# Order of the first loads and of the last token tile in a two-layer decoder trunk, on one core

## The chip, the core and the metric

The kernel runs on one core of one Trainium2 chip. A core has five engines that run side by side, each with a queue of instructions that it works off in order: TensorE (PE: matrix products, and in a part of its own the loading of the stationary operand, PEld), VectorE (DVE), ScalarE (ACT), GpSimd (POOL) and SyncE (SP, which here only issues transfers). Transfers between the device's memory (HBM) and the on-chip memory (SBUF) can be triggered from SP, ACT and POOL; a trigger is an instruction in that engine's queue. Matrix products land in PSUM, eight banks of 128 x 512 float32.

The metric is the device time of one execution in microseconds (us), as a median over runs. The kernel before was run three times: 1031.11, 1033.86 and 1035.78 us, median 1033.86.

## The reference

One sequence of 512 tokens of width 1024 goes through two layers. The first mixes tokens by a gated convolution, the second by attention in a sliding window; each is followed by a gated feed-forward part (width 2816). All is float32.

```python
def rmsnorm(x, g):
    xf = x.astype(jnp.float32)
    r = lax.rsqrt(jnp.mean(xf * xf, axis=-1, keepdims=True) + EPS)
    return (xf * r).astype(x.dtype) * g

def short_conv_mixer(h, w_in, conv_w, w_out):
    bcx = h @ w_in
    b_gate, c_gate, u = jnp.split(bcx, 3, axis=-1)
    y = b_gate * causal_depthwise_conv3(c_gate * u, conv_w)
    return y @ w_out

def swiglu(h, w_gate_up, w_down):
    g, u = jnp.split(h @ w_gate_up, 2, axis=-1)
    return (jax.nn.silu(g) * u) @ w_down

# layer 0
mix = short_conv_mixer(rmsnorm(h, a_pre_norm[l]), a_w_in[l], a_conv_w[l], a_w_out[l])
h = h + rmsnorm(mix, a_post_norm[l])
# layer 1: keys, values and queries of rmsnorm(h), windowed attention with sinks, then
h = h + rmsnorm(attn, b_post_norm[j])
# each layer ends with
ff = swiglu(rmsnorm(h, ffn_pre_norm[l]), ffn_w_gate_up[l], ffn_w_down[l])
h = h + rmsnorm(ff, ffn_post_norm[l])
```

So every part ends the same way: a mix of 512 x 1024 is divided by its root mean square, multiplied by a weight vector and added to the stream h.

## The kernel before

**Numbers in two halves.** Products are made in a faster type (F32R, a float32 of fewer bits). Each operand is split in a high part (`hi`, an ACT copy into that type) and the rest (`lo`, a DVE subtraction), and three products hi x hi, hi x lo and lo x hi are summed in PSUM (`mm3`, lines 188 to 191). So a weight tile of 128 x 1024 costs one ACT copy and one DVE subtraction before PE can use it, and PE has three products for each tile product.

**The start (lines 211 to 226 and 645 to 677).** The token matrix comes transposed as eight tiles `xt[k]` of 128 features x 512 tokens, the first three weight tiles `first[t]` (128 x 1024 each) in pieces of 2, 2 and 4 blocks of 128 columns (`CUTS`). ACT triggers the first piece of each weight tile, SP all else: `xt[0]`, the small table `gt` of norm gains and convolution taps (32 KB), `xt[1]`, the second pieces, and so on. PE begins with `WARM` = 8 products of a matrix of ones that nobody uses (tile `idle`). ACT loads its function table at a first small activation (`warm`, line 648). Then, for each k, ACT scales and copies `xt[k]` to `xhi` (needs `gt`), DVE makes `xlo`, ACT and DVE split the weight pieces, and PE makes nine products into three PSUM banks, in the order hi x hi for the three weights, then hi x lo, then lo x hi.

**The row factors (lines 680 to 699).** The first norm is applied behind the products. The squares of the tokens give a column `cols` (128 x 4, by POOL's power function); four diagonal matrices `dg` times a matrix of ones, in float32, spread it over all partitions as `pr`, which ACT copies to `rows`.

**A closing (`close`, lines 830 to 866).** The last product of a part, with its weights in slots and its operands (here `ys`), goes over four token tiles t and two halves of 512 columns. An object `Update` holds the mix, the sums of squares `s`, `v`, `r` = v to the power -1/2, the weight vector `G` spread over 128 partitions (512 KB in SBUF) and a scrap tile `junk`. Per tile: `take` (DVE, bank + mix), `square_mix` (ACT), `scale` (DVE, times G), `mean` (DVE and POOL), `update` (DVE, h += mix x r). Then h's own norm (`square`, `mean2`, `norm`), and PE's transposes (`turn`, line 323) of the normed tile `xn`. Between, `ahead.one()` splits four weight tiles of the next part (lines 396 and 401). `Update.load` (line 243) takes two tiles of a pool of 14 (`wide`) and triggers the load of G on SP.

**The last closing (lines 1129 to 1150).** No next part follows. Tiles 0 to 2 are done by halves; in tile 3 the second half is cut in two quarters of 256 columns (`take_quarter`, line 257), so that the work after PE's last product is short. Then `scale`, `update` and the store to `out`.

**What sets the order.** Blocks under `tc.manual_schedule` keep the written order of PE, DVE, ACT and POOL within that block. Across blocks, and for SP, a planner at build time orders the instructions by its own estimate of when they are ready; it also gives tiles their places and puts in the semaphores. Loads triggered by SP and ACT share eight completion semaphores in turn.

Of the kernel before, what the change touches and what calls it, by code (L numbers as in the profile page):

```python
# [16 lines left out]
P = 128  # L17
# [24 lines left out]
WARM = 8  # L42
# [30 lines left out]
def yoco_kernel(  # L73
# [67 lines left out]
    nc.vector.memset(mhalf, -0.5)  # L141
    gt = const.tile([P, N_GAIN], F32, name="gt")
# [71 lines left out]
    CUTS = [(0, 2), (2, 4), (4, KT)]  # L214
    for t in range(3):
        nc.scalar.dma_start(first[t][:, : CUTS[0][1] * P], w_in[0, t, :, : CUTS[0][1] * P])
    for k in range(KT):
        nc.sync.dma_start(xt[k], xT[k])
        if k == 0:
            nc.sync.dma_start(gt, gains)  # L220
        for k0, k1 in CUTS[1:]:
            if k == k0 - 1:
                for t in range(3):
                    nc.sync.dma_start(first[t][:, k0 * P : k1 * P],
                                      w_in[0, t, :, k0 * P : k1 * P])
# [3 lines left out]
    class Update:  # L229
# [27 lines left out]
        def take_quarter(self, t, c, ps):  # L257

            m = self.mix[t][:, S + c : S + c + 256]
            nc.vector.tensor_tensor(out=m, in0=ps[:, :256], in1=m, op=ALU.add)  # L260
            i = 2 * t + (c > 0)
            if c:
                self.scale(t, 0)
                nc.vector.tensor_scalar(out=self.s[:, i - 1 : i], in0=self.s[:, i - 1 : i],
                                        scalar1=self.s[:, 8:9], scalar2=EPS, op0=ALU.add,
                                        op1=ALU.add)
            nc.scalar.activation(self.junk[:, c : c + 256], m, AF.Square, scale=1 / 32,
                                 accum_out=self.s[:, i : i + 1] if c else self.s[:, 8:9])
            if c:
                nc.vector.tensor_scalar(out=self.v[:, t : t + 1], in0=self.s[:, i : i + 1],  # L270
                                        scalar1=self.s[:, i - 1 : i], scalar2=None, op0=ALU.add)
                nc.gpsimd.tensor_tensor(out=self.r[:, t : t + 1], in0=self.v[:, t : t + 1],
                                        in1=mhalf[:, :1], op=ALU.pow)

        def scale(self, t, half):
            c = slice(half * S, (half + 1) * S)
            m = self.mix[t][:, c]
            nc.vector.tensor_tensor(out=m, in0=m, in1=self.G[:, c], op=ALU.mult)
# [366 lines left out]
    with tc.manual_schedule(engines=ALL):  # L645
# [6 lines left out]
        for k in range(KT):  # L652
            hi, lo = xs[k]
            nc.scalar.activation(hi, xt[k], AF.Copy, scale=g(G_APRE, k))
            nc.vector.scalar_tensor_tensor(
                out=lo, in0=xt[k], scalar=g(G_APRE, k), in1=hi.bitcast(F32),
                op0=ALU.mult, op1=ALU.subtract,
            )
            for k0, k1 in CUTS:
                if k == max(k0 - 1, 0):  # L660
                    kk = slice(k0 * P, k1 * P)
                    for t in range(3):
                        hi, lo = ws[t]
                        nc.scalar.activation(hi[:, kk], first[t][:, kk], AF.Copy)
                        nc.vector.tensor_tensor(
                            out=lo[:, kk], in0=first[t][:, kk], in1=hi[:, kk].bitcast(F32),
                            op=ALU.subtract,
                        )
            kk = slice(k * P, (k + 1) * P)
            xhi, xlo = xs[k]  # L670
            for i in range(3):
# [876 lines left out]
```

## Time and profile before

| | |
|---|---|
| three runs, us | 1031.11, 1033.86, 1035.78 |
| median, us | 1033.86 |
| the profiled execution's own time: its span, us | 1031.2 |
| mean granted TensorE clock, share of full | 0.998 |
| DMA | 244.59 MB, mean 237 GB/s |
| bytes from HBM / to HBM | 237.15 MB / 102.76 MB |

The page of the profile counts one execution from its first to its last instruction (the span). A row of a timeline has the start in us, the duration in us, the engine, the line, the operation, what is written and read, the shapes and the count; in brackets how long the engine stood idle before it and what ended that. `L673` is line 673 of the kernel. `PEq`, `SPq` and `ACTq` are an engine's sequencer, which issues transfers. A list of waits has the waiting engine and line, what it waited for, the sum in us, how often, and the longest. The chain of waits follows the work that ended last back to its releasers. A group of a line's instructions has shortest, median and longest duration in ns.

### The profile page before, as it was taken

How to read it: one execution, taken by the hardware profiler on the slowest of the kernel's cores; microseconds unless marked ns; L12 is line 12 of the kernel's file. 1: busy time of each engine (PE TensorE's matmuls, PEld its weight loads, DVE VectorE, ACT ScalarE, POOL GpSimd, SP SyncE). 2: the span in 40 equal slices, each digit the busy share in tenths (PEclk: the TensorE clock that was granted, in tenths of full speed). 3: DMA queues.
4: the chain of work that ended last, by engine and by line, in shares of the span. 5: the costliest groups of instructions: out<-in, count | busy, mean ns of one | idle time of the engine just before them, and what ended most of it. 6: DMA issues, size and time to landing. Idle time of an engine off the chain costs nothing.

```text
span 1031.2 us, 17486 instructions
## 1 busy us (share of the span) xinstructions
PE 1018.6 (99%) x6652; PEld 927.2 (90%) x6652; DVE 820.9 (80%) x1397; ACT 577.4 (56%) x1037; POOL 196.8 (19%) x259
## 2 busy tenths in 40 slices
PE   9999999999999999999999999999999999999997
PEld 7888887999999899999898888889998999989986
DVE  5666766888777978878869998688886788887786
ACT  7222543865656354566466777668565554645632
POOL 0433132102101021000122664221111010210001
PEclk9999999999999999999999999999999999999999
DMA  9897689548978789869504879975899676998732
GB/s 334 290 250 235 184 261 332 160 164 256 328 243 277 254 282 301 284 209 308 190 1 135 214 216 275 256 254 164 263 284 327 177 255 203 312 293 256 244 134 82
DMA packets 66868, 244.59 MB, mean 237 GB/s; under 512 B 7904, under 2 KB 8800, under 8 KB 55008
## 3 DMA queue, kind: packets, MB, share of 16 engines
q1 hardware_dynamic: 51616, 146.34, 38.8%
q0 software_dynamic: 14592, 96.48, 36.6%
q8 instruction: 52, 0.85, 0.3%
q10 hardware_dynamic: 576, 0.66, 0.2%
q14 instruction: 32, 0.26, 0.1%
HBM read 237.15 MB, written 102.76 MB: 330 GB/s over the span
## 4 chain that ended last, share of the span: by engine, by line
PE 91%; DVE 4%; DMA 2%; ACT 1%; issue 1%; POOL 0%; POOLq 0%; SPq 0%; DVEq 0%; ACTq 0%
PE gx L191 7%; PE gx L190 7%; PE gx L189 7%; PE gz L191 4%; PE gz L190 4%; PE gz L189 4%; PE px L189 4%; PE px L191 4%; PE pcub L191 4%; PE px L190 4%; PE pcub L189 4%; PE pcub L190 4%; PE pmix L191 2%; PE pmix L189 2%; PE pmix L190 2%; PE gy L191 2%
## 5 line engine op out<-in xcount | busy, mean ns | idle before, releaser
L455 DVE TENSOR_TENSOR wlo<-raw,whi 128x1024 fp32r<-128x1024 f32 x225 | 274.9, 1226 | 93.4 <-ACT whi L454 93.3
L454 ACT ACTIVATE whi<-raw 128x1024 fp32r<-128x1024 f32 x225 | 234.5, 1050 | 120.6 <-DVE raw L442 22.0
L189 PE MATMUL gx<-xt,whi 128*128 128x256 f32 x480 | 135.8, 283 | 0.0
L190 PE MATMUL gx<-xt,whi 128*128 128x256 f32 x480 | 135.8, 283 | 0.0
L191 PE MATMUL gx<-xt,wlo 128*128 128x256 f32 x480 | 135.8, 283 | 0.0
L523 POOL DMA_DIRECT2D hsum<-in_w_gb_dram x96 | 63.2, 743 | 160.5 <-ACT whi L454 82.3
L189 PEld LDWEIGHTS gx<-xt,whi 128*128 128x128 f32 x480 | 92.2, 192 | 0.0
L190 PEld LDWEIGHTS gx<-xt,whi 128*128 128x128 f32 x480 | 92.2, 192 | 0.0
L191 PEld LDWEIGHTS gx<-xt,wlo 128*128 128x128 f32 x480 | 92.2, 192 | 0.0
L973 ACT ACTIVATE st<-gx 128x256 f32<-128x256 f32 x80 | 30.1, 382 | 81.2 <-PE gx L191 81.2
L523 POOL DMA_DIRECT2D hsum<-hsum x32 | 25.2, 788 | 258.8 <-ACT whi L454 192.3
L189 PE MATMUL pcub<-xlo,whi 128*128 128x512 f32 x168 | 65.4, 390 | 0.0
L191 PE MATMUL pcub<-xhi,wlo 128*128 128x512 f32 x168 | 65.4, 389 | 0.0
L190 PE MATMUL pcub<-xhi,whi 128*128 128x512 f32 x168 | 65.3, 389 | 0.0
L191 PE MATMUL px<-whi,alo 128*128 128x512 f32 x120 | 46.7, 389 | 0.0
L190 PE MATMUL px<-whi,ahi 128*128 128x512 f32 x120 | 46.7, 389 | 0.0
L189 PE MATMUL px<-wlo,ahi 128*128 128x512 f32 x120 | 46.7, 389 | 0.0
L191 PE MATMUL gx<-xhi,wlo 128*128 128x256 f32 x160 | 45.3, 283 | 0.0
L189 PE MATMUL gy<-xlo,whi 128*128 128x256 f32 x160 | 45.3, 283 | 0.0
L190 PE MATMUL gy<-xhi,whi 128*128 128x256 f32 x160 | 45.3, 283 | 0.0
L191 PE MATMUL gy<-xhi,wlo 128*128 128x256 f32 x160 | 45.3, 283 | 0.0
L189 PE MATMUL gz<-xt,whi 128*128 128x256 f32 x160 | 45.3, 283 | 0.0
(262 smaller groups left out, 3118.3 us busy)
## 6 DMA issues: line engine op xcount, KB each, us to landing
hsum<-in_w_gb_dram POOLq DMA_DIRECT2D x96, 512.0 KB, 8.0
raw<-hsum SPq DMA_DIRECT2D x88, 512.0 KB, 8.1
raw<-in_w_gb_dram SPq DMA_DIRECT2D x60, 512.0 KB, 7.5
hsum<-in_w_dn_dram POOLq DMA_DIRECT2D x36, 512.0 KB, 8.6
raw<-in_w_dn_dram SPq DMA_DIRECT2D x32, 512.0 KB, 7.0
hsum<-hsum POOLq DMA_DIRECT2D x28, 512.0 KB, 5.3
raw<-in_w_in_dram SPq DMA_DIRECT2D x21, 512.0 KB, 7.5
hsum<-in_w_dn_dram POOLq DMA_DIRECT2D x12, 768.0 KB, 12.2
```

Of the source, the lines that this page charges most:

```text
L189: nc.tensor.matmul(out, whi, xlo, start=start, stop=False, **kw)
L190: nc.tensor.matmul(out, whi, xhi, start=False, stop=False, **kw)
L191: nc.tensor.matmul(out, wlo, xhi, start=False, stop=stop, **kw)
L454: self.begun = nc.scalar.activation(hi[:, :n], raw, AF.Copy)
L455: nc.vector.tensor_tensor(out=lo[:, :n], in0=raw, in1=hi[:, :n].bitcast(F32), op=ALU.subtract)
L523: nc.gpsimd.dma_start(dst, src, max_dma_last_dim=4 * 4 * S, **kw))
L973: nc.scalar.activation(s, x, AF.Copy)
```

## The change

- First loads: `gt` is triggered by POOL ahead of all else on that engine. ACT triggers five weight pieces (the three first, two of the second) and not three; `xt[1]` and `xt[2]` go ahead of SP's other pieces.
- Warming: ten idle products and not eight.
- First k-tile: the weights' first block (128 columns) is split by itself, ahead of the second, and the nine products of k = 0 have an order of their own, with two lo x hi products ahead of the hi x lo ones.
- Row factors: the four diagonals stand in one tile, which is split in two parts; two products of 512 columns with a matrix of ones in the faster type replace four in float32.
- First closing: `res.load` moves into the closing's block, ahead of its work, and triggers G on ACT's queue.
- Last token tile: `update` of tile 2 moves into tile 3, in two halves behind the take of the first half and that of the first quarter; the first half's `scale` of tile 3 goes to POOL; the last quarter's sum of squares is one DVE instruction that starts from the sum so far, in place of an ACT square and a DVE sum.

```diff
-WARM = 8
+WARM = 10
...
+    gt = const.tile([P, N_GAIN], F32, name="gt")
+    nc.gpsimd.dma_start(gt, gains)
     ident = const.tile([P, P], F32, name="ident")
     make_identity(nc, ident)
     ones = const.tile([P, P], F32, name="ones")
     nc.vector.memset(ones, 1.0)
+    ones_r = const.tile([P, P], F32R, name="ones_r")
+    nc.vector.memset(ones_r.bitcast(F32), 1.0)
...
+    def piece(queue, t, c):
+        c = slice(CUTS[c][0] * P, CUTS[c][1] * P)
+        queue.dma_start(first[t][:, c], w_in[0, t, :, c])
+
     for t in range(3):
-        nc.scalar.dma_start(first[t][:, : CUTS[0][1] * P], w_in[0, t, :, : CUTS[0][1] * P])
-    for k in range(KT):
+        piece(nc.scalar, t, 0)
+    nc.sync.dma_start(xt[0], xT[0])
+    nc.sync.dma_start(xt[1], xT[1])
+    for t in range(2):
+        piece(nc.scalar, t, 1)
+    nc.sync.dma_start(xt[2], xT[2])
+    piece(nc.sync, 2, 1)
+    nc.sync.dma_start(xt[3], xT[3])
+    for t in range(3):
+        piece(nc.sync, t, 2)
+    for k in range(4, KT):
         nc.sync.dma_start(xt[k], xT[k])
-        if k == 0:
-            nc.sync.dma_start(gt, gains)
-        for k0, k1 in CUTS[1:]:
-            if k == k0 - 1:
-                for t in range(3):
-                    nc.sync.dma_start(first[t][:, k0 * P : k1 * P],
-                                      w_in[0, t, :, k0 * P : k1 * P])
...
-        def load(self):
+        def load(self, queue=nc.sync):
             self.G, self.junk = wide("G"), wide("junk")
-            nc.sync.dma_start(self.G, behind[self.gain].partition_broadcast(P))
+            queue.dma_start(self.G, behind[self.gain].partition_broadcast(P))
...
-            i = 2 * t + (c > 0)
-            if c:
-                self.scale(t, 0)
-                nc.vector.tensor_scalar(out=self.s[:, i - 1 : i], in0=self.s[:, i - 1 : i],
-                                        scalar1=self.s[:, 8:9], scalar2=EPS, op0=ALU.add,
-                                        op1=ALU.add)
-            nc.scalar.activation(self.junk[:, c : c + 256], m, AF.Square, scale=1 / 32,
-                                 accum_out=self.s[:, i : i + 1] if c else self.s[:, 8:9])
-            if c:
-                nc.vector.tensor_scalar(out=self.v[:, t : t + 1], in0=self.s[:, i : i + 1],
-                                        scalar1=self.s[:, i - 1 : i], scalar2=None, op0=ALU.add)
-                nc.gpsimd.tensor_tensor(out=self.r[:, t : t + 1], in0=self.v[:, t : t + 1],
-                                        in1=mhalf[:, :1], op=ALU.pow)
+            i = 2 * t
+            if not c:
+                nc.scalar.activation(self.junk[:, S : S + 256], m, AF.Square, scale=1 / 32,
+                                     accum_out=self.s[:, 8:9])
+                return
+            nc.vector.tensor_scalar(out=self.s[:, i : i + 1], in0=self.s[:, i : i + 1],
+                                    scalar1=self.s[:, 8:9], scalar2=EPS, op0=ALU.add,
+                                    op1=ALU.add)
+            nc.vector.tensor_tensor_reduce(out=self.junk[:, S : S + 256], in0=m, in1=m,
+                                           scale=1 / D, scalar=self.s[:, i : i + 1],
+                                           op0=ALU.mult, op1=ALU.add,
+                                           accum_out=self.v[:, t : t + 1])
+            nc.gpsimd.tensor_tensor(out=self.r[:, t : t + 1], in0=self.v[:, t : t + 1],
+                                    in1=mhalf[:, :1], op=ALU.pow)
...
+        token_hi(0)
+        for t in range(3):
+            first_hi(t, 0, 1)
+        first_lo(0, 0, 1)
+        first_lo(1, 0, 1)
+        token_lo(0)
+        first_lo(2, 0, 1)
+        for t in range(3):
+            first_hi(t, 1, 2)
+        products(0, [(0, 0), (0, 1), (0, 2), (2, 0), (2, 1), (1, 0), (1, 1), (1, 2), (2, 2)])
+        for k in range(1, KT):
+            token_hi(k)
+            token_lo(k)
             for k0, k1 in CUTS:
-                if k == max(k0 - 1, 0):
+                if k == max(k0 - 1, 1):
...
+            products(k, [(i, t) for i in range(3) for t in range(3)])
...
+        dg, dhi, dlo = slot("dg"), slot("dhi", F32R), slot("dlo", F32R)
         for b in range(NB):
-            dg = slot("dg", w=P)
-            nc.vector.tensor_scalar(out=dg, in0=ident, scalar1=cols[:, b : b + 1], scalar2=None,
-                                    op0=ALU.mult)
-            nc.tensor.matmul(pr[:, b * P : (b + 1) * P], ones, dg, start=True, stop=True)
+            nc.vector.tensor_scalar(out=dg[:, b * P : (b + 1) * P], in0=ident,
+                                    scalar1=cols[:, b : b + 1], scalar2=None, op0=ALU.mult)
+        nc.scalar.activation(dhi, dg, AF.Copy)
+        nc.vector.tensor_tensor(out=dlo, in0=dg, in1=dhi.bitcast(F32), op=ALU.subtract)
+        nc.tensor.matmul(pr, ones_r, dlo, start=True, stop=False)
+        nc.tensor.matmul(pr, ones_r, dhi, start=False, stop=True)
...
     res = Update(mix_c, B_CONV, [G_FPRE[0]])
     res.leaves = True
-    res.load()
...
         issue(len(issues))
+        res.load(nc.scalar)
         close(ws, ys, 0, res, ahead)
...
                             res.take_quarter(t, c, ps)
+                            if not c:
+                                res.update(t - 1, S, D)
+                                nc.sync.dma_start(out[t - 1], hs[t - 1])
...
                         res.square_mix(t, half)
+                        if t == NB - 1:
+                            res.update(t - 1, 0, S)
+                            res.scale(t, 0, nc.gpsimd)
...
-                for c in range(0, D, D if t < NB - 1 else S):
-                    e = c + (D if t < NB - 1 else S)
-                    res.update(t, c, e)
-                    (nc.sync if c == 0 else nc.scalar).dma_start(out[t, :, c:e],
-                                                                 hs[t][:, c:e])
+                if t < NB - 2:
+                    res.update(t)
+                    nc.sync.dma_start(out[t], hs[t])
+            for c, queue in ((0, nc.sync), (S, nc.scalar)):
+                res.update(NB - 1, c, c + S)
+                queue.dma_start(out[NB - 1, :, c : c + S], hs[NB - 1][:, c : c + S])
```

More of the change, by code (lines that the diff above doesn't have):

```diff
@@ L655, in yoco_kernel, with token_hi, token_lo, products @@
+        def token_hi(k):
+            nc.scalar.activation(xs[k][0], xt[k], AF.Copy, scale=g(G_APRE, k))
+        def token_lo(k):
             nc.vector.scalar_tensor_tensor(
-                out=lo, in0=xt[k], scalar=g(G_APRE, k), in1=hi.bitcast(F32),
+                out=xs[k][1], in0=xt[k], scalar=g(G_APRE, k), in1=xs[k][0].bitcast(F32),
                 op0=ALU.mult, op1=ALU.subtract,
             )
+        def products(k, passes):
+            kk = slice(k * P, (k + 1) * P)
+            for i, t in passes:
+                whi, wlo = ws[t]
+                nc.tensor.matmul(begun[0][t], (whi, whi, wlo)[i][:, kk],
+                                 xs[k][i == 1], start=k == i == 0,
+                                 stop=k == KT - 1 and i == 2)
@@ L662, in yoco_kernel @@
                     for t in range(3):
[L663 to L671, printed above, removed]
-                for ps, (whi, wlo) in zip(begun[0], ws):
-                    nc.tensor.matmul(ps, (whi, whi, wlo)[i][:, kk], (xhi, xlo, xhi)[i],
-                                     start=k == i == 0, stop=k == KT - 1 and i == 2)
+                        if k0:
+                            first_hi(t, k0, k1)
@@ L675, in yoco_kernel @@
+                    for t in range(3):
+                        first_lo(t, max(k0, 1), k1)
+            products(k, [(i, t) for i in range(3) for t in range(3)])
         later += [fetch(w_in[1, t]) for t in range(len(later), 3)]
```

16 lines of the change are left out of this document (9 added, 7 removed).

## The prediction

> **What bounds the kernel now.** I read the page's busy shares first, then the list of what TensorE (PE) waited for, over the whole span.
>
> ```profile
> span 1031.2 us, 17486 instructions
> PE 1018.6 (99%) x6652; PEld 927.2 (90%) x6652; DVE 820.9 (80%) x1397; ACT 577.4 (56%) x1037; POOL 196.8 (19%) x259
> ...
> PE xt L323 <- ACT xn L312: 2.8, 1, 2.8
> PE idle L651 <- DVE mhalf L141: 1.1, 1, 1.1
> PE pcub L673 <- ACT whi L664: 0.8, 1, 0.8
> PE psc L1239 <- DVE nm L1251: 0.6, 2, 0.3
> ```
>
> PE is the bound: it is busy for 1018.6 of 1031.2 us and stands still by 2.8 us once (in the first closing), by some 2 us at the start, and after its last product. A change can win only where PE waits, runs slowly, does needless work, or is done. The change touches one place of each kind, and since PE hardly waits elsewhere, what is won early should arrive at the end. The page's own time is a span of 1031.2 us; the three runs lie at 1031.11 to 1035.78 with a median of 1033.86, so 2.7 us above it. I work out a difference from the span and take it off the median.
>
> **The start.** The timeline of the first 24 us:
>
> ```profile
> 0.74 1.37 ACTq L216 DMA_DIRECT2D raw<-in_w_in_dram  x3
> 1.06 3.79 PE L651 MATMUL idle<-ones 128*128 128x128 f32 x16 [1.06 <-DVE mhalf L141]
> 1.18 0.42 SPq L220 DMA_DIRECT2D gt<-in_gains_dram  x1
> 2.14 1.28 ACT L648 ACT_TABLE_LOAD   x1 [2.14 <-issue]
> 4.57 0.72 ACT L654 ACTIVATE xhi<-xt,gt 128x512 fp32r<-128x512 f32 x1 [0.93 <-DMA gt<-in_gains_dram]
> 5.20 1.13 ACT L664 ACTIVATE whi<-raw 128x256 fp32r<-128x256 f32 x3
> 5.65 1.65 PE L673 MATMUL pcub<-xhi,whi 128*128 128x512 f32 x3 [0.81 <-ACT whi L664]
> ...
> 9.53 0.86 PE L673 MATMUL pcub<-xhi,whi 128*128 128x512 f32 x3
> ...
> 11.61 0.84 PE L673 MATMUL pcub<-xhi,whi 128*128 128x512 f32 x3
> ```
>
> The first nine real matmuls take 5.65 to 9.53 (0.431 us each), the next nine 9.53 to 11.61 (0.231). So nine at the slow pace cost 9 x 0.200 = 1.80 us. The warming ran 3.79 us, to 4.85, and stopped 0.8 us before the first product; then 3.9 us without a break brought the quick pace (the views' granted clock shows no dip there, so the pace is read from the starts). Ten warming matmuls in place of eight, at 3.79/8 = 0.47 each, run to 5.8.
>
> The first product: ACT still begins xhi at about 4.57, if gt has landed and ACT is free. Two more triggers on ACT at 1.37/3 = 0.46 move the table load from 2.14 to 3.06 and the small activation behind it to 4.34-4.55, which hides in the wait of today. The first weight piece has 128 columns and not 256: 0.3 for 0.4. So PE can begin at 5.5, before the warming ends, and the pause is gone. If an unbroken run brings the quick pace, it comes about 4 us after 1.06, near the first products; I keep two slow matmuls (0.4). The gain: 0.15 + 1.80 - 0.40 = 1.55 us; bounds 0 (the pace changes at 9.4 as now) and 1.95. The feed holds: at 0.231 a k-tile needs 2.1 us of PE, and ACT 0.72 + 3 x 0.38 = 1.9 for its pieces, DVE about as much. xt[2], the tenth load of both queues now, becomes one of the first eight.
>
> The Trainium skill (TensorE: Matmul & The Clock Gate, Part 1: The HAM clock gate) has the clock double after one busy window of about 3.4 us whose phase is free. By that rule an unbroken run from 1.06 switches between 4.5 and 7.9 us, and my term would be 0.8 to 1.95, different from run to run; the rows above agree with it as far as one run can.
>
> **gt by POOL's queue.** Its trigger is POOL's first instruction of the kernel; the other queues' first triggers begin at 0.74, and I take that for POOL.
>
> ```profile
> hsum<-in_w_gb_dram POOLq DMA_DIRECT2D x96, 512.0 KB, 8.0
> raw<-in_w_gb_dram SPq DMA_DIRECT2D x60, 512.0 KB, 7.5
> hsum<-in_w_dn_dram POOLq DMA_DIRECT2D x12, 768.0 KB, 12.2
> ```
>
> On SP gt takes 3.3 us (triggered at 1.18, and the wait for it ends at about 4.5). No small load on POOL's queue is in the trace; the same source takes 8.0 there and 7.5 on SP, 0.5 more. From below 0.74 + 3.3 = 4.04, from above 0.74 + 8.0 = 8.74. I take 0.74 + 3.3 + 0.5 = 4.54, in time for ACT, because gt has 32 KB and the 8.0 is for 512.
>
> **rows by two matmuls.**
>
> ```profile
> 27.11 0.88 DVE L695 TENSOR_SCALAR dg<-ident,cols 128x128 f32<-128x128 f32 x4 [1.15 <-POOL cols L690]
> 34.73 1.05 PE L697 MATMUL pr<-dg,ones 128*128 128x128 f32 x8
> 35.54 0.47 PE L189 MATMUL pcub<-xlo,whi 128*128 128x512 f32 x1
> 35.82 0.60 ACT L698 ACTIVATE rrow<-pr 128x512 f32<-128x512 f32 x1 [4.66 <-PE pr L697]
> ```
>
> Eight matmuls hold PE from 34.73 to 35.54, 0.81 us; two of 512 columns at 0.23 take 0.45: 0.36 us won (0 to 0.4). The added split is one ACT copy (0.60, by the row of rrow) and one DVE subtraction (0.69, as L278 below). dg is done at 27.99, so they end by 30, before PE's 34.73; ACT stands idle 4.66 us there. Without that cover they would cost 1.3. The ones_r memset (some 0.1 on DVE) is hidden in the loads.
>
> **The norm weights G at the first closing.**
>
> ```profile
> 159.11 1.23 DVE L401 TENSOR_TENSOR wlo<-raw,whi 128x1024 fp32r<-128x1024 f32 x1
> 161.64 0.69 DVE L737 TENSOR_TENSOR ylo<-bry,yhi 128x512 fp32r<-128x512 f32 x1 [0.70 <-ACT yhi L736]
> 162.13 0.39 PE L189 MATMUL pmix<-wlo,yhi 128*128 128x512 f32 x1
> ...
> 155.76 13.33 DMA G<-in_behind_dram
> 169.18 0.69 DVE L278 TENSOR_TENSOR mix<-mix,G 128x512 f32<-128x512 f32 x1 [4.78 <-DMA G<-in_behind_dram]
> 181.51 1.86 PE L323 MATMUL xt<-ident,xn 128*128 128x128 f32 x15 [2.77 <-ACT xn L312]
> ...
> G<-in_behind_dram SPq DMA_DIRECT2D x4, 512.0 KB, 5.8
> ```
>
> SP issues G at 155.76, among loads for the feed-forward part, and it takes 13.33 us where the median of the four G loads is 5.8. DVE idles 4.78 us for it, the chain of scale, mean, update and norm runs late, and PE's transposes stand 2.77 us. On ACT's queue nothing is ahead of G, and it is ACT's first instruction of the closing; issued at 155 it lands at 161 by the median, and 166.4 (169.18 - 2.77) is enough. What stands behind the trigger on ACT: the four weight conversions (L396), and on DVE their rests (L401, 1.23 each); SP's raw loads wait for those. Their weights belong to the feed-forward part, whose products come after the transposes at 181.51, so that is covered, but each rest that slides behind 155 pushes DVE's work for the last y (L737 ends at 162.33), and PE needs it at 162.13 already. Bounds: 2.77 won, or all of it eaten by two or three rests (2.5 to 3.7): 2.77 to -0.9. I take 2.3, since today all four rests are done before L737 (the last starts at 159.11) without a wait of PE, and most of that work fits between DVE's own waits.
>
> **The last token tile.**
>
> ```profile
> 1024.19 0.42 DVE L260 TENSOR_TENSOR mix<-pmix,mix 128x256 f32<-128x256 f32 x1 [0.58 <-PE pmix L191]
> 1024.53 0.68 DVE L278 TENSOR_TENSOR mix<-mix,G 128x512 f32<-128x512 f32 x1
> 1025.44 0.21 DVE L270 TENSOR_SCALAR uv<-us 128x1 f32<-128x1 f32 x1
> 1025.73 0.93 POOL L272 TENSOR_TENSOR ur<-uv,mhalf 128x1 f32<-128x1 f32 x1 [4.38 <-DVE uv L270]
> 1026.70 1.42 DVE L290 SCALAR_TENSOR_TENSOR h<-mix,ur,h 128x512 f32<-128x512 f32 x2 [0.44 <-POOL ur L272]
> ...
> L1251 DVE CUSTOM_DVE_ANT_0 s<-psc,mask,nsnk x64: 330/472/487, 558.2 to 652.1; 128x256 f32<-128x256 f32 x48, 128x128 f32<-128x128 f32 x16
> L1251 DVE DVE_READ_ACCUMULATOR2_ANT nm<- x64: 71/80/90, 558.5 to 652.5; 128x1 f32 x64
> ...
> L732 POOL TENSOR_TENSOR bry<-cut,bry x3: 1290/1291/3267, 93.1 to 144.4; 128x512 f32<-128x512 f32 x3
> ```
>
> From the last take (1024.61) to the power on POOL (1025.73) stand now a scale, the square on ACT and two small sums. After it stand a small sum (0.21) and a product with sum, priced by the mask operation of the attention: 0.47 + 0.08. Each starts some 0.08 before the one ahead of it ends (1024.53 against 1024.61), so with 0.07 to POOL the power begins at 1024.61 + 0.21 + 0.55 - 0.16 + 0.07 = 1025.28: 0.45 us won, and everything behind it follows. The second scale (0.68) lies under the power (0.93). The update of tile 2, moved into the last tile, uses DVE while PE still works on the last products; its store leaves SP about 1 us later than now (its second half waits for the first quarter's take), ahead of the last tile's stores, which leave after 1026.9. The first half's scale goes to POOL: 1.29 us from about 1022.8, done by 1025. If it takes 3.27 as L732 once did, it ends at 1026.07 and the power waits: 0.35 lost. Bounds -0.35 to 0.55.
>
> The sum: 1.55 + 0.36 + 2.3 + 0.45 = 4.7 us off the span, 1026.5; off the median, **1029.2**.
>
> **Rival 1, ACT is held by its fifth trigger.**
>
> ```profile
> DMA to landing us min/median/max: 3.5/3.5/4.2
> ...
> 2.59 0.43 SPq L224 DMA_DIRECT2D raw<-in_w_in_dram  x1
> 4.29 0.33 SPq L224 DMA_DIRECT2D raw<-in_w_in_dram  x1
> ```
>
> Above are the landings of ACT's three loads, and SP's fifth and sixth trigger. The eighth load of both queues goes at 2.59, the ninth only at 4.29, just when the first has landed (0.74 + 3.5 = 4.24). If ACT's fifth load becomes the ninth, the table load starts at 4.65, xhi at 6.2, and the first product at 7.1, 1.45 late. With the quick pace by then it is 0.35 to the good, without it 1.45 to the bad; the middle, 0.55 lost, gives -0.55 + 3.1 = 2.6 and 1031.3. For it: both queues trigger at one rate (0.45), and ACT, SP, ACT, SP makes it the ninth. Against: gt has left SP's list, and in the program's order it is the seventh.
>
> **Rival 2, G lands no earlier, or the last y takes its place.** The closing gives nothing: 1.55 + 0.36 + 0.45 = 2.4, 1031.5. For it: the zero slack at 162.13, and the three other G loads, which do not show whether queue or traffic made the 13.33. The Trainium skill (DMA: Bandwidth & Descriptors, Issuing engines are not separate DMA queues) says that loads of all issuing engines share the same sixteen DMA engines, and that another issuer saves the issue time alone; by that rule this rival's 1031.5 stands, and no run here shows it yet. Against it: on ACT's queue G waits behind no other load, only beside them.
>
> **Rival 3, slower: gt is late on POOL's queue.** Then each us late is a us lost, and the pause returns with the slow pace. The rest wins 3.1, so this decides from a landing at 4.48 + 3.1 = 7.6. At 8.74 it costs 4.3 and gives 1035.0; with 12.2 us (the longest row) 8.5 and 1039.2. Against it: 32 KB.
>
> **How the numbers follow.** Forecast 0.47, rival 1 0.25, rival 2 0.15, rival 3 0.08, and 0.05 that the planner's new order of SP's and POOL's transfers costs a wait that I have not priced. Half a per cent (5.2 us: 1028.7 and 1039.0) is about what a measurement of this kernel can tell from no change. Less than half of the forecast's case lies below 1028.7 (all upper bounds together give 5.7), with a little of the rivals: faster 0.31. Slower takes rival 3's far end and half of the unpriced: 0.06. Same 0.63. The range goes from 1026.0 (5.7 and 2 us of the runs' scatter) to 1034.5 (short of rival 3).
>
> **What will show it.** Right: no gap between the last idle matmul and the first product at 5.5-5.9, matmuls 0.23 apart by 7 us; gt landed by 4.6; G landed by 166 and no wait of PE before L323; POOL's power begins 0.7 us after the last take's end and not 1.1. Wrong: ACT's table load after 4 us (rival 1), G past 166 or a gap of PE near 162 (rival 2), xhi waiting for gt past 7 (rival 3), POOL's scale longer than 2.4 us.

## The result, and the profile after

| | before | after |
|---|---|---|
| runs beside each other | 13 | 13 |
| median, us (range) | 1033.59 (1031.11 to 1038.75) | 1033.01 (1031.15 to 1035.13) |
| ratio, 95% interval | | 0.9988 [0.9976, 1.0000] |
| profiled execution: span, us | 1031.2 | 1033.2 |
| mean granted clock in it | 0.998 | 0.994 |

The medians differ by 0.6 us, the ratio makes it 1.2 (its interval 0 to 2.5); 4.7 were forecast. A run's time is some 1.8 us above its span (1034.99 and 1033.2 for the profiled run of after). The profiled execution of after is one of its two slowest runs, 2.0 us longer than the profiled one of before, so what is peculiar to it has to be told apart from what every run has. The start of the page, and what PE waited for in the whole span:

```profile
span 1033.2 us, 17488 instructions
PE 1019.7 (99%) x6650; PEld 928.4 (90%) x6650; DVE 823.5 (80%) x1403; ACT 576.9 (56%) x1039; POOL 196.7 (19%) x261
...
PE xt L334 <- ACT xn L323: 2.2, 1, 2.2
PE pcub L686 <- ACT whi L666: 2.0, 1, 2.0
```

The wait at the transposes has shrunk from 2.8 to 2.2 only, and the one ahead of the first product has grown from 0.8 to 2.0. The timeline of the start:

```profile
0.74 2.37 ACTq L221 DMA_DIRECT2D raw<-in_w_in_dram  x5
1.06 3.87 PE L662 MATMUL idle<-ones 128*128 128x128 f32 x20 [1.06 <-DVE ones L141]
1.29 0.74 POOL L137 DMA_DIRECT2D gt<-in_gains_dram  x1 [0.84 <-POOLq L1583]
3.15 1.28 ACT L659 ACT_TABLE_LOAD   x1 [3.15 <-issue]
5.99 0.72 ACT L674 ACTIVATE xhi<-xt,gt 128x512 fp32r<-128x512 f32 x1 [1.34 <-DMA gt<-in_gains_dram]
6.96 1.32 PE L686 MATMUL pcub<-xhi,whi 128*128 128x512 f32 x3 [2.03 <-ACT whi L666]
8.07 1.06 PE L686 MATMUL pcub<-xhi,wlo 128*128 128x512 f32 x2
8.92 1.49 PE L686 MATMUL pcub<-xlo,whi 128*128 128x512 f32 x3
```

POOL's trigger begins at 1.29 and gt is there 4.7 us later, at 5.96. ACT, free since 4.64, waits for it. The warming ends at 4.93, PE stands 2.03 us, and the products from 7.4 on run at half the pace of those just before. The windows view gives the granted clock (the third number from the end) beside PE's busy time (the second number), here in stretches of 3.41 us that follow the clock's own changes in this execution:

```profile
0.55:3.96 3.41, 2.90 (x13) 2.90 (x14) 0.32 (x3) 0.81 (x1) 1.26 (x3) 1.00 0.56 150
3.96:7.38 3.42, 1.39 (x11) 1.17 (x10) 0.44 (x3) 2.07 (x7) 0.00 (x0) 1.00 1.07 370
7.38:10.79 3.41, 3.41 (x10) 2.76 (x9) 3.16 (x10) 3.41 (x10) 0.00 (x0) 0.50 0.94 288
178.04:181.46 3.42, 1.41 (x7) 0.89 (x5) 2.61 (x6) 3.36 (x7) 1.13 (x2) 1.00 1.01 424
181.46:184.87 3.41, 3.23 (x16) 3.23 (x16) 2.74 (x5) 1.55 (x4) 0.34 (x1) 0.50 0.90 370
```

Twice a stretch in which PE was busy for 1.39 or 1.41 us (41%) is followed by one at half clock. That costs up to 1.7 us each time (half of 3.41, where PE works throughout). This is what is peculiar to this execution: the first of the two is in none of the six later profiles that start as after does (kernels 2 to 7 below). The second one makes the fifteen transposes last 3.41 us where before had 1.86. Now the chain of waits through the first closing:

```profile
150.41 17.06 DMA hsum<-in_w_gb_dram
167.47 0.29 issue
167.75 2.80 POOL hsum L534 x5
170.55 0.61 POOL ur L296
171.16 0.02 issue
171.19 1.29 DVE h L301
...
180.55 1.05 ACT xn L323
181.59 0.05 issue
181.64 3.41 PE xt L334 x15
```

G is no longer in it: triggered at 147.26 and 11.2 us on its way, it lands at 158.4, 10.7 earlier than before. In its place stand POOL's own triggers for partial sums (`hsum`: blocks of the next part's weights, added up by transfers from HBM to HBM), the last five of which wait for a sum that lands at 167.47. The power `ur` stands behind them in POOL's queue. The same was so before, in rows of the timeline that the prediction did not read:

```profile
167.15 0.79 POOL L523 DMA_DIRECT2D hsum<-in_w_gb_dram  x1 [1.05 <-DMA hsum<-in_w_gb_dram]
167.67 2.28 POOL L523 DMA_DIRECT2D hsum<-in_w_dn_dram  x4
170.08 0.94 POOL L285 TENSOR_TENSOR ur<-uv,mhalf 128x1 f32<-128x1 f32 x1
```

The last row has no bracket, so POOL was not idle ahead of the power: it had just finished its triggers (167.67 + 2.28 = 169.95), in the same tenth of a us in which DVE, late by G, had the sum ready (169.79 + 0.21 = 170.00). Two things were late there together. Last, the end of after, DVE and POOL:

```profile
1023.66 0.74 DVE L301 SCALAR_TENSOR_TENSOR h<-mix,ur,h 128x512 f32<-128x512 f32 x1
...
1024.64 1.30 POOL L289 TENSOR_TENSOR mix<-mix,G 128x512 f32<-128x512 f32 x1 [1.54 <-ACT junk L264]
1024.83 1.66 DVE L301 SCALAR_TENSOR_TENSOR h<-mix,ur,h 128x512 f32<-128x512 f32 x1
1026.40 0.41 DVE L270 TENSOR_TENSOR mix<-pmix,mix 128x256 f32<-128x256 f32 x1
1026.97 0.48 DVE L279 CUSTOM_DVE_ANT_0 junk<-mix,us 128x256 f32<-128x256 f32 x1
1027.54 1.05 POOL L283 TENSOR_TENSOR ur<-uv,mhalf 128x1 f32<-128x1 f32 x1 [1.61 <-DVE uv L279]
```

PE's last product (the timeline's row begins at 1025.60 and takes 0.28) ends at 1025.88. The last take starts only at 1026.40: DVE is held by an update of 1.66 us whose other half (first row) took 0.74. From the last product to the end of the span it is 7.33 us, where it was 7.08.

### The profile page after: what moved, and what is told of

Same layout as the page of the kernel before. It is cut to its first block, busy times and chain, and to the rows that moved or that the text cites. A ratio compares the mean times of both kernels' runs of the same rounds, so it can differ in the third digit from the quotient of the medians.

```text
span 1033.2 us, 17488 instructions
## 1 busy us (share of the span) xinstructions
PE 1019.7 (99%) x6650; PEld 928.4 (90%) x6650; DVE 823.5 (80%) x1403; ACT 576.9 (56%) x1039; POOL 196.7 (19%) x261
## 4 chain that ended last, share of the span: by engine, by line
PE 89%; DVE 4%; DMA 4%; ACT 1%; issue 1%; POOL 1%; POOLq 0%; DVEq 0%; ACTq 0%
PE gx L194 7%; PE gx L193 7%; PE gx L192 7%; PE gz L194 4%; PE gz L193 4%; PE gz L192 4%; PE px L193 3%; PE px L192 3%; PE px L194 3%; PE pcub L194 3%; PE pcub L192 3%; PE pcub L193 3%; DMA hsum<-in_w_gb_dram 3%; PE pmix L192 2%; PE pmix L193 2%; PE pmix L194 2%
```

## The experiments

Each kernel is the changed kernel with the edit shown; each is compared with runs of the kernel before on the same chip, whose medians there were 1033.94 (for 1 to 4), 1034.38 (5 to 8), 1034.51 (9 to 11) and 1033.63 (12). The ratio is an estimate from all these runs and not the quotient of the two medians. The intervals of 1 to 8 overlap that of after, so what each of these edits does is read from the rows of its profile and not from its total; those of 9 to 12 lie clear below. The last four columns are of its profiled execution, in us: the pause ahead of the first product, the start of the first closing's products (pmix), PE's wait at the transposes there, and the stretch from the last product to the end.

| kernel | median | ratio to before, 95% | pause | pmix | wait | end |
|---|---|---|---|---|---|---|
| before | 1033.59 | | 0.81 | 158.05 | 2.8 | 7.08 |
| after | 1033.01 | 0.9988 [0.9976, 1.0000] | 2.03 | 158.77 | 2.2 | 7.33 |
| 1 gt on SP | 1032.07 | 0.9990 [0.9976, 1.0005] | 0 | 156.53 | 1.8 | 7.30 |
| 2 late sums | 1031.10 | 0.9978 [0.9964, 0.9991] | 0.96 | 157.10 | 1.1 | 7.33 |
| 3 scale on DVE | 1033.65 | 0.9994 [0.9978, 1.0010] | 1.67 | 157.12 | 2.8 | 7.12 |
| 4 G ahead of the block | 1034.89 | 1.0013 [0.9996, 1.0029] | 1.37 | 157.09 | 2.7 | 7.33 |
| 5 = 2 and 4 | 1032.11 | 0.9971 [0.9953, 0.9988] | 0.96 | 156.91 | 1.0 | 7.34 |
| 6 = 2, G on SP | 1035.19 | 1.0003 [0.9987, 1.0019] | 1.48 | 157.02 | 2.3 | 7.33 |
| 7 last tile's order | 1032.57 | 0.9986 [0.9966, 1.0005] | 1.28 | 156.98 | 2.1 | 6.86 |
| 8 warming of 16 | 1031.49 | 0.9975 [0.9959, 0.9991] | 0 | 157.41 | 1.7 | 7.34 |
| 9 = 1, 2, 4, 7 | 1029.22 | 0.9951 [0.9938, 0.9963] | 0 | 156.28 | 0.5 | 6.81 |
| 10 = 1, 2, 7 | 1029.86 | 0.9957 [0.9945, 0.9969] | 0 | 156.29 | 1.1 | 6.80 |
| 11 = 10, G between | 1028.26 | 0.9941 [0.9928, 0.9954] | 0.42 | 156.51 | 0 | 6.82 |
| 12 = 11, warming of 8 | 1029.79 | 0.9961 [0.9948, 0.9973] | 0.74 | 157.71 | 0 | 6.82 |

**1. gt on SP**

```diff
-    nc.gpsimd.dma_start(gt, gains)
...
     nc.sync.dma_start(xt[0], xT[0])
+    nc.sync.dma_start(gt, gains)
```

> The changed kernel with gt triggered on SP again, behind xt[0], as before the change; all else stays. Theory (gt on POOL's queue is late): gt lands at 4.4 to 4.6 instead of 5.96, xhi starts at 4.6 to 4.7 instead of 5.99, the first product at 5.5 to 5.7 instead of 6.96, PE's wait before it is 0.6 to 0.8 instead of 2.03, and the granted clock has no half-speed stretch after 4 us; pcub's products come 0.23 apart from the start, and pr's products start at 34.0 to 34.4 instead of 35.87. Rival (the loads share the sixteen DMA engines, so gt's queue does not matter): gt or the weight pieces still land near 6, first product at 6.5 to 7. Rival (xt[1] or the second pieces come late instead, as SP's list is longer by one): first product at 5.6, but gaps of PE of 0.5 or more by 9 us, and pr not before 35. Total: the wait of PE in the first closing takes back most of what the start wins, so 0 to 1.5 us below the changed kernel; if PE's wait there is not tied to anything fixed, 1.5 to 1.9 below.

ACT and PE in its timeline:

```profile
4.56 0.72 ACT L674 ACTIVATE xhi<-xt,gt 128x512 fp32r<-128x512 f32 x1
5.54 1.34 PE L686 MATMUL pcub<-xhi,whi 128*128 128x512 f32 x3
```

gt landed at 4.47, and neither row has a wait ahead of it. The row factors' products started at 33.63 (35.87 in after, 34.73 before), earlier than the 34.0 to 34.4 expected; no pause was left at all. As nothing else was changed, gt's queue was the cause. The total did not show it: the ratio is that of after, and POOL's triggers still held PE for 1.8 us in the closing, with 0.7 more in a later one at 685.

**2. Late sums**

```diff
-        sum_on("o1")
-        issue(len(issues))
         res.load(nc.scalar)
         close(ws, ys, 0, res, ahead)
+        sum_on("o1")
+        issue(len(issues))
```

> The changed kernel with the second half of the partial sums (their DMA triggers on POOL and POOL's additions, which at the first closing stand ahead of POOL's first power) moved behind the closing; G stays on ACT. Theory (POOL's first power for tile 0 waits behind POOL's triggers, which wait for a sum that lands at 167.5): the power starts right after its sum of squares, at 168.5 to 169.2 instead of 170.30, and PE's wait at the transposes falls from 2.2 to 0.5 to 1.2; the last product ends 1 to 1.7 us earlier, unless the sums are then late for the next part (a wait of PE at the silu or the products behind 182). Rival (the conversions of the next part's weights, moved behind the load of G, set the end of the takes and with them the transposes): the wait stays at 1.8 or more. Rival (the start's delay): nothing changes in the closing.

POOL in its closing:

```profile
167.44 0.95 POOL L296 TENSOR_TENSOR ur<-uv,mhalf 128x1 f32<-128x1 f32 x1 [17.48 <-DVE uv L292]
```

POOL now waits for DVE's sum and not the other way round; PE's wait fell to 1.1 as expected, and no wait came up behind it. What is left of the wait is DVE's, whose rows are

```profile
160.37 4.63 DVE L412 TENSOR_TENSOR wlo<-raw,whi 128x1024 fp32r<-128x1024 f32 x4 [0.26 <-ACT whi L407]
164.91 1.28 DVE L259 TENSOR_TENSOR mix<-pmix,mix 128x512 f32<-128x512 f32 x2
```

The first take is at 164.91 (163.02 before), behind the four splits of the next weights that the change pushed behind G's trigger.

**3. The scale on DVE**

```diff
-                            res.scale(t, 0, nc.gpsimd)
+                            res.scale(t, 0)
```

> The changed kernel with the first scale of the last token tile on DVE instead of POOL. Theory (POOL's product of two SBUF operands and DVE's update of tile 2 slow each other): the update's half behind that scale takes 0.70 to 0.80 instead of 1.66, POOL's 1.30 goes and DVE's 0.68 comes; the last take starts 0.0 to 0.1 behind the last product instead of 0.5, and the stretch from the last product to the end of the span is 6.9 to 7.0 us instead of 7.33. Rival (DVE has too much work between the last products, whichever engine scales): the update is 0.75 but the take waits 0.2 to 0.5 for the scale, and the stretch stays at 7.2 to 7.5.

DVE in its last tile, after a last product that ended at 1025.15:

```profile
1024.48 0.42 DVE L270 TENSOR_TENSOR mix<-pmix,mix 128x256 f32<-128x256 f32 x1
1024.81 0.74 DVE L301 SCALAR_TENSOR_TENSOR h<-mix,ur,h 128x512 f32<-128x512 f32 x1
1025.47 0.42 DVE L270 TENSOR_TENSOR mix<-pmix,mix 128x256 f32<-128x256 f32 x1
```

The update is back to 0.74, so it was POOL's scale that stretched it. But the take is 0.32 late, and the end 7.12 and not 6.9 to 7.0: the work in front of it is too much in this order, as the rival had it, only less so.

**4 to 6. G's place and the sums.** In 4 G's load stands ahead of the hand-ordered block:

```diff
+    res.load(nc.scalar)
     sum_on("o0")
...
-        res.load(nc.scalar)
```

> The changed kernel with G's load still on ACT's queue, but ahead of the block with the hand-written order, so that ACT's and DVE's splits of the next part's weights need not stand behind its trigger. Theory (POOL's late power sets the transposes, G is no longer it): the splits return to 142 to 160, the first take to about 163, G lands by 166, and POOL's power still starts at 169.9 to 170.4 and PE still waits 1.8 to 2.4 at the transposes. Rival (the splits behind the trigger set it): PE's wait falls below 1. Rival (ahead of the block the planner puts the trigger late or early in traffic, so G lands past 167): DVE waits for G and PE's wait is 2.5 or more.

5 adds the late sums of 2:

> The changed kernel with both edits of the closing: G's load on ACT's queue ahead of the hand-ordered block, and the second half of the partial sums behind the closing. In the six profiles so far PE's wait at the transposes is the start of POOL's first power less the first pmix product less 9.3 us, to within 0.1. Theory (three things were late there: G, POOL's triggers, and DVE's splits; with the first two out of the way the third goes too): the first take lies at 162 to 163, G lands 8 to 10 us after the first pmix product or earlier, the power starts 9.0 to 9.9 us after the first pmix product, and PE waits 0 to 0.6 at the transposes, with no half-speed stretch behind it. Rival (G's landing is set by the traffic, as the sixteen DMA engines are full from 144 to 180): G lands at 165.5 or later and PE waits 0.7 or more. The total is then 1.0 to 2.5 below the changed kernel's median.

6 is 5 with `res.load()`, which triggers on SP as before the change:

> The changed kernel with the second half of the partial sums behind the closing and G's load on SP again, at its place before the change. Theory (G and POOL's triggers were both late before, so moving either one alone does little): G lands at 167 to 169 again and PE's wait at the transposes is 2 to 3 us although POOL is free. Rival (only POOL's triggers ever mattered): the wait is 1.2 or less, as with G on ACT. Rival (with the sums out of the traffic G lands early on SP as well): G by 166 and the wait below 1; then G's queue is of no use and its place among the loads is all.

POOL's rows of 4, in which its triggers run up to the power:

```profile
167.10 2.29 POOL L534 DMA_DIRECT2D hsum<-in_w_dn_dram  x4
169.13 0.86 POOL L296 TENSOR_TENSOR ur<-uv,mhalf 128x1 f32<-128x1 f32 x1
```

DVE's first scale in 5:

```profile
166.31 0.69 DVE L289 TENSOR_TENSOR mix<-mix,G 128x512 f32<-128x512 f32 x1 [3.05 <-DMA G<-in_behind_dram]
```

and in 6:

```profile
167.62 0.69 DVE L289 TENSOR_TENSOR mix<-mix,G 128x512 f32<-128x512 f32 x1 [4.27 <-DMA G<-in_behind_dram]
```

In 4 the splits are early again, the takes at 162.07 and G at 166.2, yet PE waits 2.7 (1.8 to 2.4 expected), since POOL's triggers hold the power until 169.13. In 5 POOL is free, but ahead of the block the trigger came only at 156.9 and G at 166.2: the theory's 0 to 0.6 was missed (1.0), and its rival had the landing right. In 6 POOL is free and G on SP lands at 167.5: the wait is 2.3. So each of the three can hold the transposes when the other two are out of the way or less late: G (6), POOL's triggers (4), DVE's splits (2). In all twelve profiles in which PE waits there, the wait is the start of the power less the first pmix product less 9.3 us, within 0.1.

**7. The last tile's order**

```diff
                             res.take_quarter(t, c, ps)
                             if not c:
-                                res.update(t - 1, S, D)
-                                nc.sync.dma_start(out[t - 1], hs[t - 1])
+                                res.scale(t, 0)
...
-                            res.update(t - 1, 0, S)
-                            res.scale(t, 0, nc.gpsimd)
+                            res.update(t - 1)
+                            nc.sync.dma_start(out[t - 1], hs[t - 1])
```

> The changed kernel with another order of the last token tile: tile 2's whole update directly behind tile 3's first take, and tile 3's first scale on DVE, between the takes of its two quarters. Theory (the last take was late by DVE's work between the last products; the sums behind the take are 0.4 shorter, as was forecast): the last take starts at most 0.15 behind the last product's end, the power starts 1.15 behind the take, and the stretch from the last product to the end is 6.8 to 6.95 (7.33 in the changed kernel, 7.08 before, 7.12 with the scale on DVE but the update in halves). Rival (DVE is short of time in whatever order): the take is 0.3 or more late and the stretch 7.1 or more.

DVE and POOL behind a last product that ended at 1022.91:

```profile
1020.69 1.28 DVE L301 SCALAR_TENSOR_TENSOR h<-mix,ur,h 128x1024 f32<-128x1024 f32 x1
1022.22 0.68 DVE L289 TENSOR_TENSOR mix<-mix,G 128x512 f32<-128x512 f32 x1
1022.95 0.42 DVE L270 TENSOR_TENSOR mix<-pmix,mix 128x256 f32<-128x256 f32 x1
1024.10 1.05 POOL L283 TENSOR_TENSOR ur<-uv,mhalf 128x1 f32<-128x1 f32 x1 [3.98 <-DVE uv L279]
```

The take is 0.04 late, the power 1.15 behind it, the end 6.86: as expected. The total, 1032.57, does not show these 0.5 us against after.

**8. A warming of 16**

```diff
-WARM = 10
+WARM = 16
```

> The changed kernel with 16 warming products instead of 10, gt still on POOL's queue. Theory (the granted clock is decided in fixed stretches of 3.41 us: one in which PE is busy for about 41% or less is followed by one at half speed; the pause of 2.03 us before the first product did that in the changed kernel's profile, pauses of 0.96 to 1.67 in three others did not): the pause shrinks to 0 to 0.9, no half-speed stretch follows the start, the first product still starts at 6.6 to 7.0, and pr's products start at 34.1 to 34.4 instead of 35.87. Rival (the half-speed stretch comes from something else, the traffic or the first products themselves): it is there in spite of the filled pause. Rival (the warming now runs past the operands): the first product starts past 7.2.

PE at its start:

```profile
1.06 6.39 PE L662 MATMUL idle<-ones 128*128 128x128 f32 x32 [1.06 <-DVE ones L141]
7.21 0.94 PE L686 MATMUL pcub<-xhi,whi 128*128 128x512 f32 x3
```

No pause and no half-speed stretch. The warming runs a little past the operands (first product at 7.21 for 6.6 to 7.0, just what the last rival had), which costs some 0.3 to 0.5 us: the row factors' products start at 34.51 (34.1 to 34.4 expected), where kernels 2 to 7 had 34.02 to 34.23, and 35.87 in after.

**9 to 11. The edits together.** 9 is 1, 2, 4 and 7; 10 leaves G as the block's first instruction; 11 puts it behind the second split (shown against 10):

```diff
             ahead.one()
             ahead.one()
+            if half == 0 and then:
+                then(nc.scalar)
...
-        res.load(nc.scalar)
-        close(ws, ys, 0, res, ahead)
+        close(ws, ys, 0, res, ahead, res.load)
```

> The changed kernel with four edits together: gt on SP behind xt[0], G on ACT's queue ahead of the hand-ordered block, the second half of the partial sums behind the closing, and the last tile's order with the whole update and DVE's scale between the quarters. Theory (the effects are local and add): first product at 5.5 to 5.7 without a pause, pr at 33.6 to 33.9, PE's wait at the transposes 0.8 to 1.2 (G triggered at 156 to 157 and landing 9 us later sets it), the stretch behind the last product 6.8 to 6.95, no half-speed stretch before the end; span 1028.0 to 1028.6 in an undisturbed execution, and a median 2.5 to 4 below the kernel before. Rival (the early part is bound by the sixteen full DMA engines, so that the start's gain is taken back by a longer wait at the transposes): the wait is 1.8 or more and the span 1029 or more.

> As the other run with four edits, but G's load stays the first instruction of the hand-ordered block on ACT, as in the changed kernel. Theory: G is triggered at about 145 and lands by 157, the splits of the next part's weights stand behind it (159 to 163), the first take is at 164 to 165 and PE's wait at the transposes is 1.0 to 1.3, as with the late sums alone; span 1028.0 to 1028.6. Rival (as DVE's splits are now the last thing late, an earlier start makes them no earlier): the wait grows by what the start won, to 1.8 or more.

> As the other two runs with four edits, but G's load is put on ACT's queue behind the second of the four splits of the next part's weights: two of them stand ahead of its trigger and two behind. Theory (each of G, POOL's triggers and DVE's splits must be early, or the transposes wait): G is triggered at 148 to 150 and lands by 162, the first take is at 162 to 163.5, POOL's first power starts 8.5 to 9.6 us after the first pmix product, and PE waits 0 to 0.4 at the transposes; span 1027.2 to 1027.9. Rival (the traffic decides, and G or a raw weight tile lands late wherever it is triggered): the wait is 0.8 or more.

DVE and POOL of 11 in the closing:

```profile
162.05 1.28 DVE L259 TENSOR_TENSOR mix<-pmix,mix 128x512 f32<-128x512 f32 x2
163.52 0.69 DVE L289 TENSOR_TENSOR mix<-mix,G 128x512 f32<-128x512 f32 x1 [0.19 <-ACT junk L264]
164.58 0.94 POOL L296 TENSOR_TENSOR ur<-uv,mhalf 128x1 f32<-128x1 f32 x1 [15.05 <-DVE uv L292]
```

G was triggered at 146.3 and not at 148 to 150, landed at 157.3, and the power starts 8.1 us after the first pmix product: PE does not wait there any more. 9 and 10 waited 0.5 and 1.1, so the three places of G rank as their waits do. The single gains stand side by side in the table: no pause or a short one, a short wait or none, an end of 6.8. The totals of 9 and 10 came out lower than expected: spans of 1027.1 and 1027.8 for 1028.0 to 1028.6, and 9's median 5.3 below before for 2.5 to 4; why is open, beyond 9's wait of 0.5 for 0.8 to 1.2. 11, with a span of 1027.3 as expected, has the lowest median of all, 5.9 per mille below before by the ratio. What it keeps is 0.8 us in the closing at 682, where the chain shows POOL's triggers for sums ahead of the power once more. Its six runs, and those of 9 and of 10, lie within 0.7 to 1.1 us of each other; the 13 of after spread over 4.0.

**12. As 11, with 8 warming products**

> The kernel with gt on SP, G behind the second split, late sums and the mended last tile, with 8 warming products as before the change instead of 10. Theory (the quick pace opens at the end of a fixed stretch of 3.41 us that PE was nearly wholly busy in; a stretch that was 76% busy did not open it, one of 85% did): the warming ends at 4.7 to 4.95 and a pause of 0.5 to 0.8 stands ahead of the first product, so in some executions the pace opens at 4.5 to 5 or past 5.5 and in others only at 8 to 9.4; pr then starts at 33.4 to 35.0, the median lies 0.3 to 1.2 above the run with 10 products (1028.26) and the runs spread more than its 1.1 us. Rival (two more warming products bring nothing, it is gt and the order of the loads that count): median within 0.25 of 1028.26 and the same spread.

PE's first two stretches of 3.41 us in the windows view, and PE in the timeline:

```profile
2.70:6.11 3.41, 2.67 (x12) 2.35 (x11) 0.54 (x3) 2.60 (x5) 0.00 (x0) 1.00 0.99 321
6.11:9.53 3.42, 3.42 (x9) 2.44 (x8) 2.65 (x8) 3.19 (x10) 0.00 (x0) 1.00 0.94 276
```

```profile
5.59 1.71 PE L686 MATMUL pcub<-xhi,whi 128*128 128x512 f32 x3 [0.74 <-ACT whi L666]
...
9.60 0.86 PE L686 MATMUL pcub<-xhi,whi 128*128 128x512 f32 x3
```

The first stretch is 78% busy and the pace stays slow; the second is full, and at 9.53 it doubles. pr starts 1.20 later than in 11 and the span is 1.2 longer. The median is 1.53 higher (more than the 1.2 expected), though 12 ran on another chip, on which the kernel before was 0.9 faster; the runs spread over 2.3 us. The longer warming was worth its two products.

## Why the prediction was wrong, step by step

The median lies in the range and within half a per cent of before, as was likeliest, but 3.8 us above the forecast.

**The start (1.55 forecast).** The step that failed is gt's landing, put at 0.74 + 3.3 + 0.5 = 4.54. POOL's first trigger began at 1.29 and not at 0.74, and gt took 4.7 us in the profile of after, 4.3 to 4.5 in seven others, and not 3.8, so it landed at 5.6 to 6.0. That is rival 3's mechanism at a third of its price of 4.3; its turning point of 7.6 was not reached. With gt back on SP (kernel 1) the rest of the step held nearly: first product at 5.54 (5.5 forecast), quick pace before 7, the second token tile's products 1.42 us earlier than before (8.11 against 9.53), the row factors' 1.10 (1.35 and 1.34 in kernels 9 and 10). What took the last 0.3 of it in kernel 1 is open; PE shows no wait between. With gt on POOL the gain was 0.5 to 0.7 (kernels 2 to 7), and a loss of 1.1 where the pause fell into one stretch of the clock. Rival 1 did not happen: the table load came at 3.15.

**The row factors (0.36).** Right: two products from 35.87 to 36.33, 0.46 against 0.81.

**The closing (2.3).** The step that failed is that 2.77 us of PE's standing were G's alone. G did come early, as meant; 8.5 of its 10.7 us are the earlier trigger, the rest a shorter journey. But POOL's triggers, which the sum left out, ended within 0.1 us of G's effect before. They wait for a sum that was 17.06 us on its way, while the DMA engines were full (from 144 to 180 a busy share of 1.03 before and 1.02 after); that the full engines made it late is not shown. The danger that was weighed, the splits sliding behind the trigger, came true too (takes at 166.59), hidden behind POOL. So PE's wait shrank by 0.6 in this profile, by 0.7 to 1.1 in those of 1, 7 and 8, and not at all in that of 3, all with the same closing. Rival 2 (the closing gives nothing) came nearest, with POOL's power in the place that it gave to the last y. The Trainium skill (DMA: Bandwidth & Descriptors, Issuing engines are not separate DMA queues) has another issuer save the issue time alone. For G the rows agree: ACT had triggered nothing since its first five loads, and G was still 11.2 us on its way, where the forecast had the median of 5.8. For gt they do not: 3.3 us on SP's queue (kernel 1) and 4.7 on POOL's, whose trigger is only 0.3 longer (0.74 against 0.42).

**The last tile (0.45).** The sums behind the take are shorter as forecast: from the take's start to the power's 1.14 us, 1.54 before. What failed is the sentence that the moved update uses DVE while PE still works: beside POOL's scale it took 1.66 for 0.74 and made the take 0.5 late, and the power itself took 1.05 for 0.93. Instead of 0.45 won, 0.25 was lost. In kernel 7, with the cover in order, 0.22 was won: 0.39 ahead of the power, of which the power itself, 1.05 there too, took back 0.12.

**The sum.** For an execution without half-speed stretches, from kernels 3, 4 and 7, whose start (and in 3 and 7 whose closing) is that of after: the closing begins 0.9 to 1.1 us earlier, PE's wait there is 0 to 0.7 shorter, and the end costs 0.25, which makes 0.7 to 1.5; the medians show 0.6, the ratio 1.2.

## What to carry to other kernels

Where an engine waits for one thing, look up what the next instruction of every engine in that chain was doing in the same microsecond: a row without an idle time ahead of it may be a second thing that is late, and then removing the first one alone wins only the difference. Arithmetic that others wait for should not stand behind transfer triggers which themselves wait for loads. And a short wait of PE can be worth more than its length when it falls into one clock stretch: count it with the half-speed stretch that may follow.

## What the runs showed of the hardware

**The clock.** In all fourteen profiles the granted clock changes only on a grid of 3.41 us, whose phase differs from execution to execution. With the clock up, stretches in which PE was busy for 38% (kernel 3) and 41% (after, twice) were followed by half clock, those of 46% (1), 49% (8), 51% (3) and more were not. At the start, where the view shows 1.00 throughout and the clock is read from the pace of the products, stretches of 76% (before) and 78% (12) did not raise it, one of 85% (after) did. So a pause of about 2 us (59% of 3.41) is enough, if the grid lies badly. After's wait of 2.2 fell into one stretch (41% busy); kernel 7's of 2.1 was split over two (63% and 74%) and before's of 2.8 too (62% and 56%), and neither was followed by half clock. By these rows the same wait can cost 2 us in one run and up to 3.7 in the next. One half-speed stretch takes 0.5 x 3.41 / 1030 = 0.0017 off a mean clock of some 0.998. Runs at 0.996 or less were 5 of 12 for kernel 3 and 6 of 12 each for 4 and 6, whose waits at the transposes are 2.3 to 2.8, and 26 of 91 for the kernel before (2.8); 2 of 13 for after and 3 of 12 for 7 (2.2 and 2.1); 3 of 12 for 1 and 1 of 12 for 8 (1.8 and 1.7); 1 of 12 for 2 and none of 12 for 5 (1.1 and 1.0); none of 24 for 9 to 12. That goes with the scatter of the times; it was not tried by itself. The Trainium skill (TensorE: Matmul & The Clock Gate, Part 1: The HAM clock gate) has the same window, free-running, but lets the clock fall after a window that is idle; here it fell after one that was 41% busy.

**DVE beside POOL.** A DVE product with sum of two SBUF operands took 1.66 us instead of 0.74 beside a POOL product, and 0.74 again in kernel 3, where POOL's was gone. It started 0.19 after POOL's and ended 0.55 after it (1026.49 against 1025.94). The Trainium skill (SBUF — State Buffer, Who interferes with whom) has a VectorE instruction with two SBUF inputs contend with a GpSimd instruction that reads SBUF, under an exclusive lock. The rows agree in that DVE's instruction needed 0.55 more when POOL's was done, most of the 0.74 that it takes alone.
